# One transfer instead of two for the first tile of a streamed mixture of softmaxes, and a buffer wait moved from ScalarE to GpSimd

## The chip, the cores and the metric

The kernel runs on one core of a Trainium2 chip. The metric is device time in microseconds (us). I also give the **span** of the profiled execution, the time from its first to its last recorded work.

## The reference, cut to what matters

```python
batch, seq, vocab, num_heads = 32, 128, 4096, 4
# logits [32, 128, 4, 4096] fp32, prior [32, 128, 4] fp32
prior_probs = softmax(prior, axis=-1)
mixture = np.sum(prior_probs[..., None] * softmax(logits, axis=-1), axis=2)   # [32, 128, 4096]
```

For each of 4096 rows: four softmaxes over 4096 numbers, weighted and added. 268.5 MB are read and 67.1 MB written.

## The kernel before

The rows are worked on in U = 32 units of 128 rows, one row to a partition. A unit reads 64 KB a row (four heads of 16 KB) and writes 16 KB a row. The input tile holds two units, so unit u's load goes where unit u - 2 was.

```python
    def load(u):
        if u == 0 or u >= U - 3:
            cuts = (0, 2, 3, 4) if u == U - 1 else (0, 2, 4)
        else:
            cuts = (0, H)
        for h, to in zip(cuts, cuts[1:]):
            ld = nc.scalar.dma_start(
                out=ltile[:, u % 2, h:to], in_=lg[u // J, u % J, :, h:to, :]
            )
            if u >= 2:
                only(ld, adds[u - 2, 0] if h == 0 else exps[u - 2, to - 1])
            # ...
            for k in range(h, to):
                loads[u, k] = ld
```

`only` says what an instruction waits for. Loads are issued from ScalarE's queue, most stores from SyncE's, so they are two queues on the same 16 DMA engines (the page of the kernel before books 82.2% and 17.6% of the 16 engines' time on them). In each unit:

```python
            def exp(h, *keep):                      # ScalarE: exponential and its sum
                ex = nc.scalar.activation(es[h], lt[:, h], AF.Exp, accum_out=dsum[:, u, h : h + 1])
                keep = (loads[u, h],) + keep
                if bufd and u and h in (1, 2):      # the buffers of unit u - 1 must be free
                    keep += (adds[u - 1, 1 if h == 1 else H - 1],)
                exps[u, h] = only(ex, *keep)

            def weigh(h, n, *keep):                 # VectorE reciprocal, GpSimd product
                # ...
                return only(mul, rc, *keep)

            free = (stores[u - 2],) if bufd and u >= 2 else ()     # the output tile of unit u - 2
            # ... sets: ((0, H),) for u < U - 4, then pairs and singles of heads
            for h in range(H):
                if h == 2 and 0 < u < U - 3:
                    store(u - 1, obuf[:, (u - 1) % 2], nc.sync)
                # ...
                exp(h, *(free if sets[0][1] == H and h == H - 1 else ()))
                # ...
                mul = weigh(g, h + 1 - g, *(free if g == 0 and h < H - 1 else ()))
                for k in range(g, h + 1):           # VectorE: scale head 0, then add 1 to 3
                    # ... add(k, mul, ...)
```

So load u + 2 waits for the scaling of unit u (`adds[u, 0]`), which waits for all four exponentials of unit u.

The softmax here doesn't subtract the row's maximum and nothing guards it: scores larger than these inputs give would overflow.

## Time and profile before

| | before |
|---|---|
| time, median | 780.8 us |
| span | 779.1 us |
| moved | 335.64 MB, 431 GB/s over the span |
| VectorE, ScalarE, GpSimd busy | 66%, 61%, 1% |
| DMA engines | full from the first load to the end |

The table says that transfers are the bound: no compute engine is busy for more than two thirds of the span, and the DMA row of the profile is full.

### The profile page before, as it was taken

The numbers are of one execution on the slowest core, as the hardware profiler recorded it, in microseconds if no ns is written. First come the engines' busy times: TensorE is split into PE (matmuls) and PEld (weight loads), VectorE is DVE, ScalarE is ACT, GpSimd is POOL, SyncE is SP. The second block draws the span as 40 slices with busy tenths as digits, with TensorE's granted clock in tenths as the row PEclk, the third lists the DMA queues.
The fourth block names the chain that finished last, engine by engine and source line by source line (L and its number), as shares of the span: only waits on it lengthen the run. The fifth ranks groups of instructions, "written<-read, shape, count | busy, mean of one in ns | idle before, by whom it ended". The sixth has DMA issues, their size and how long they took to land.

```text
span 779.1 us, 620 instructions
## 1 busy us (share of the span) xinstructions
DVE 517.7 (66%) x175; ACT 472.2 (61%) x258; POOL 7.6 (1%) x41
## 2 busy tenths in 40 slices
DVE  2447865568655686556875558755577555788986
ACT  4376555765557755577555675556755567557782
POOL 0000000000000000000000000000000000000000
DMA  9999999999999999999999999999999999999998
GB/s 407 458 417 400 475 404 431 431 465 424 404 468 401 463 417 423 452 448 414 417 468 407 458 404 468 421 413 448 416 459 417 457 405 464 410 429 431 432 428 379
DMA packets 10131, 335.64 MB, mean 431 GB/s; under 512 B 1136, under 2 KB 1136, under 8 KB 1168
## 3 DMA queue, kind: packets, MB, share of 16 engines
q10 hardware_dynamic: 6048, 276.83, 82.2%
q1 hardware_dynamic: 4080, 58.79, 17.6%
q14 instruction: 3, 0.02, 0.0%
HBM read 268.50 MB, written 67.11 MB: 431 GB/s over the span
## 4 chain that ended last, share of the span: by engine, by line
DMA 60%; DVE 28%; ACT 9%; issue 2%; POOL 0%; DVEq 0%; ACTq 0%; POOLq 0%
DMA out_dram<-obuf 47%; DVE obuf L200 23%; DMA ltile<-in_logits_dram 13%; ACT ebuf L176 8%; DVE obuf L194 4%; DVE ltile L200 1%; ACT ltile L176 1%; POOL coeff L187 0%; DVE rden L185 0%; DVEq L271 0%; ACTq L111 0%; POOLq L271 0%; ACTq L176 0%
## 5 line engine op out<-in xcount | busy, mean ns | idle before, releaser
L200 DVE SCALAR_TENSOR_TENSOR obuf<-ebuf,coeff,obuf 128x4096 f32<-128x4096 f32 x90 | 403.6, 4484 | 3.8 <-POOL coeff L187 0.6
L176 ACT ACTIVATE ebuf<-ltile 128x4096 f32<-128x4096 f32 x90 | 324.1, 3601 | 33.3 <-DVE obuf L200 19.4
L176 ACT ACTIVATE ltile<-ltile 128x4096 f32<-128x4096 f32 x38 | 137.4, 3615 | 255.4 <-DMA ltile<-in_logits_dram 255.0
L185 DVE RECIPROCAL rden<-dsum 128x4 f32<-128x4 f32 (+2 forms) x37 | 6.4, 174 | 235.9 <-ACT ebuf L176 233.2
L194 DVE TENSOR_SCALAR obuf<-ltile,coeff 128x4096 f32<-128x4096 f32 x30 | 70.6, 2353 | 10.9 <-POOL coeff L187 10.9
L200 DVE SCALAR_TENSOR_TENSOR ltile<-ltile,coeff 128x4096 f32<-128x4096 f32 (+1 forms) x7 | 27.0, 3874 | 1.0 <-POOL coeff L187 0.9
L176 ACT ACTIVATION_READ_ACCUMULATOR ebuf<-ltile 128x1 f32 x90 | 16.8, 187 | 0.0
L187 POOL TENSOR_TENSOR coeff<-rden,pp 128x4 f32<-128x4 f32 (+2 forms) x37 | 7.4, 201 | 756.2 <-DVE rden L185 745.6
L176 ACT ACTIVATION_READ_ACCUMULATOR ltile<-ltile 128x1 f32 x38 | 7.1, 186 | 0.0
L194 DVE TENSOR_SCALAR ltile<-ltile,coeff 128x4096 f32<-128x4096 f32 x2 | 4.7, 2353 | 0.6 <-POOL coeff L187 0.6
L153 ACT ACT_TABLE_LOAD x1 | 1.3, 1283 | 2.2 <-issue 2.2
L151 DVE TENSOR_REDUCE pmax<-pr 32x128 f32<-32x512 f32 x1 | 0.7, 674 | 2.5 <-DMA pr<-in_prior_dram 2.5
L162 DVE STREAM_TRANSPOSE pp<-pn 32x256 f32<-32x256 f32 x4 | 1.7, 435 | 0.1
L154 DVE TENSOR_REDUCE pmax<-pr 32x128 f32<-32x512 f32 x1 | 0.7, 674 | 0.7 <-ACT pr L153 0.7
L156 DVE TENSOR_TENSOR pn<-pr,pmax 32x512 f32<-32x512 f32 x1 | 1.0, 1019 | 0.0
L155 DVE RECIPROCAL pmax<-pmax 32x128 f32<-32x128 f32 x1 | 0.9, 941 | 0.0
L153 ACT ACTIVATE pr<-pr 32x512 f32<-32x512 f32 x1 | 0.6, 628 | 0.5 <-DVE pr L152 0.5
L152 DVE TENSOR_TENSOR pr<-pr,pmax 32x512 f32<-32x512 f32 x1 | 0.7, 679 | 0.0
L260 POOL MEMSET const-bfloat16-1.0<- 128x1 bf16 x1 | 0.1, 102 | 0.0
L260 POOL MEMSET const-uint8-127<- 128x1 uint8 x1 | 0.1, 102 | 0.0
L260 POOL MEMSET const-float32-0.0<- 128x1 f32 x1 | 0.1, 99 | 0.2 <-issue 0.2
L260 POOL MEMSET const-float32-1.0<- 128x1 f32 x1 | 0.1, 99 | 0.0
## 6 DMA issues: line engine op xcount, KB each, us to landing
out_dram<-obuf SPq DMA_DIRECT2D x28, 2048.0 KB, 28.1
ltile<-in_logits_dram ACTq DMA_DIRECT2D x7, 4096.0 KB, 25.5
ltile<-in_logits_dram ACTq DMA_DIRECT2D x2, 2048.0 KB, 30.9
out_dram<-obuf ACTq DMA_DIRECT2D x2, 2048.0 KB, 26.6
out_dram<-ltile ACTq DMA_DIRECT2D x1, 2048.0 KB, 19.3
out_dram<-ltile ACTq DMA_DIRECT2D x2, 1024.0 KB, 4.8
ltile<-in_logits_dram ACTq DMA_DIRECT2D x28, 29.6
pr<-in_prior_dram SPq DMA_DIRECT2D x1, 64.0 KB, 2.5
```

The lines of the kernel that those rows point to most:

```text
L151: nc.vector.reduce_max(pmax, pr, axis=AX.X)
L152: nc.vector.tensor_sub(pr, pr, pmax.unsqueeze(2).to_broadcast([2 * G, P, H]))
L153: nc.scalar.activation(pr, pr, AF.Exp)
L154: nc.vector.reduce_sum(pmax, pr, axis=AX.X)
L155: nc.vector.reciprocal(pmax, pmax)
L156: nc.vector.tensor_mul(pn.rearrange("k h r -> k r h"), pr, pmax.unsqueeze(2).to_broadcast([2 * G, P, H]))
L162: nc.vector.transpose(pp[32 * t : 32 * (t + 1), :, :, c : c + 2 * G], pq[:, :, :, 32 * (t % 2) : 32 * (t % 2 + 1)],)
L176: ex = nc.scalar.activation(es[h], lt[:, h], AF.Exp, accum_out=dsum[:, u, h : h + 1])
L185: rc = nc.vector.reciprocal(rden[:, u, h : h + n], dsum[:, u, h : h + n])
L187: mul = nc.gpsimd.tensor_mul(coeff[:, u, h : h + n], rden[:, u, h : h + n], ppu[:, h : h + n])
L194: st = nc.vector.tensor_scalar(out=acc[:, lo:hi], in0=es[h][:, lo:hi], scalar1=coeff[:, u, h : h + 1], scalar2=None, op0=ALU.mult,)
L200: st = nc.vector.scalar_tensor_tensor(out=acc[:, lo:hi], in0=es[h][:, lo:hi], scalar=coeff[:, u, h : h + 1], in1=acc[:, lo:hi], op0=ALU.mu ...
```

## The change

Its intent: fewer and larger transfers at the start, and ScalarE freed from a wait on a store in the two units where GpSimd may take it.

```diff
     def load(u):
-        if u == 0 or u >= U - 3:
+        if u >= U - 3:
             cuts = (0, 2, 3, 4) if u == U - 1 else (0, 2, 4)
...
-                exp(h, *(free if sets[0][1] == H and h == H - 1 else ()))
+                exp(h, *(free if 4 <= u < U - 4 and h == H - 1 else ()))
...
-                mul = weigh(g, h + 1 - g, *(free if g == 0 and h < H - 1 else ()))
+                mul = weigh(g, h + 1 - g, *(free if g == 0 and not 4 <= u < U - 4 else ()))
```

## The prediction

> **What bounds the kernel now.** I read the page of the kernel before first: shares by engine, then the row of DMA slices.
>
> ```profile
> span 779.1 us, 620 instructions
> ...
> DVE 517.7 (66%) x175; ACT 472.2 (61%) x258; POOL 7.6 (1%) x41
> ...
> DMA  9999999999999999999999999999999999999998
> ...
> DMA packets 10131, 335.64 MB, mean 431 GB/s; under 512 B 1136, under 2 KB 1136, under 8 KB 1168
> ```
>
> No compute engine reaches 70%, while the DMA engines are at 9 tenths or more in 39 of 40 slices and 8 in the last. The reference has to read 268.5 MB and write 67.1 MB, and the kernel moves just that. The transfers are the bound; compute only has to issue them in time.
>
> Next, the chain of waits in order of time, for the steady rate. A piece of the middle:
>
> ```profile
> 120.33 28.15 DMA out_dram<-obuf
> 148.50 3.72 ACT ebuf L176 x2
> ...
> 152.73 2.37 DVE obuf L194
> 155.12 4.50 DVE obuf L200
> 159.64 4.50 DVE obuf L200
> 164.16 4.50 DVE obuf L200
> 168.68 28.44 DMA out_dram<-obuf
> ```
>
> The columns are start, length, what. A unit is 128 rows of 64 KB in (8.39 MB) and 16 KB out (2.10 MB), so 10.49 MB. The chain repeats every 168.68 - 120.33 = 48.35 us, and that is two units (its links go from unit u to u + 2, through the store that frees an output buffer). So 20.97 MB go in 48.35 us: 434 GB/s, or **24.17 us a unit**. The 28 us of a 2 MB store are no slow store: it shares the engines with the next unit's load. At 434 GB/s all 335.64 MB need 773.4 us of the 779.1 us span. Only some 5.7 us are start, end and lost rate, so no change that moves the same bytes can win more than that.
>
> The second number is what compute alone would need per unit. The third add of unit u frees the PSUM tile and the last buffer for the exponentials 2 and 3 of unit u + 1. The loop is therefore: three adds (13.53 us), two exponentials (about 3.72 each with the accumulator read, 7.4 together), reciprocal, GpSimd product and their gaps (103.67 + 0.19 to 104.38, 0.5 us), the scaling on VectorE (2.35 and 0.04 of gap): **23.8 us**. Compute is faster than the transfers by 0.37 us a unit. That is the rate at which a compute delay is made up.
>
> Last, the timeline of the first 60 us, where the change acts.
>
> ```profile
> 12.25 3.62 ACT L176 ACTIVATE ltile<-ltile 128x4096 f32<-128x4096 f32 x1 [7.70 <-DMA ltile<-in_logits_dram]
> ...
> 21.96 3.59 ACT L176 ACTIVATE ebuf<-ltile 128x4096 f32<-128x4096 f32 x1 [2.40 <-DMA ltile<-in_logits_dram]
> ...
> 32.18 0.33 ACTq L111 DMA_DIRECT2D ltile<-in_logits_dram  x1
> 32.18 13.53 DVE L200 SCALAR_TENSOR_TENSOR obuf<-ebuf,coeff,obuf 128x4096 f32<-128x4096 f32 x3
> 41.31 3.62 ACT L176 ACTIVATE ltile<-ltile 128x4096 f32<-128x4096 f32 x1 [12.04 <-DMA ltile<-in_logits_dram]
> ...
> 58.73 0.33 ACTq L111 DMA_DIRECT2D ltile<-in_logits_dram  x1
> ```
>
> Unit 0's first half is there at 12.2 us, its second at 21.9, unit 1 at 41.3. Load 2 is issued at 32.18, when the scaling of unit 0 has freed its buffer, 9.1 us before load 1 is in: that is the lead the change will spend.
>
> **What the Trainium skill says.** "Perfetto Trace Analysis", section DMA Optimizations: splitting a transfer may let work start sooner "if DMA engines are generally idle". Here they are not, yet the split does start ScalarE sooner (12.25 rather than 21.96); the question is whether anybody needs that. "DMA: Bandwidth & Descriptors", section Queues, rings and completion order: each engine takes turns between its queues by packets. The trace agrees: the packet records show store 0, issued at 45.74, starting its first data packet at 50.57, amid load 2's packets. Same page, section Latency and other measured facts: a first byte about 0.6 us after the issue on the queues of SyncE and ScalarE. The trace shows more: unit 0's load begins issue at 0.12 and its first packet starts at 1.29, so I take 1.2 us. Same page, section Where 436 GB/s comes from: a ceiling of 435.2 GB/s. The 434 above agrees, and leaves nothing to gain in rate.
>
> **The change part by part.**
>
> *One load for unit 0.* It removes one DMA issue (0.33 us of ScalarE's queue) and leaves bytes and order alike: 8.39 MB, then unit 1. Unit 0 should land at 21.9 us as before. ScalarE then does four exponentials after 21.9 instead of two. Unit 1 shows what that takes: from 41.31 to the end of the scaling at 58.73, 17.42 us. So load 2 is issued at 21.96 + 17.42 = **39.4 us instead of 32.18: 7.2 us later**. Now follow the transfers:
> - Load 1's last packets end at 40.4 to 40.9 us. Load 2's first can start at 39.4 + 1.2 = 40.6. So the engines idle for about 0 to 0.3 us. The lead of 9.1 us shrinks to 1.9, still about what an issue takes.
> - Unit 0's adds end at 39.4 + 13.55 = 52.9 (before 45.74), and store 0 follows. Exponential 2 of unit 1 waits for it (before: no wait, 48.52). So unit 1's scaling ends at 39.4 + 23.8 = 63.2 instead of 58.73, and load 3 is issued 4.5 us later.
> - From 40.6 the engines have load 2 and store 0, 10.49 MB: busy until 40.6 + 24.17 = 64.8. Load 3 can start at 63.2 + 1.2 = 64.4. No gap, by 0.4 us: what covers it is store 0, which now is mostly sent after load 2.
> - From there each round takes 23.8 us of compute against 24.17 of transfers, so the margin grows by 0.37 a unit. Unit 3's scaling would end at 39.4 + 3 x 23.8 = 110.8 (before 106.77), 4.0 us late, and the delay is gone after 4.0 / 0.37, some 11 units, about unit 14. From there the two kernels should look alike, the end included.
>
> So 7.2 us of delay on ScalarE cost 0 to 0.3 us of span at the first joint and perhaps 0 to 0.4 at the second.
>
> *The wait for the output tile, units 2 and 3.* It moves from the fourth exponential to GpSimd's product, which runs after that exponential anyway. Nothing is added. Before, unit 2 did not wait, and unit 3 waited this long:
>
> ```profile
> 100.14 3.62 ACT L176 ACTIVATE ebuf<-ltile 128x4096 f32<-128x4096 f32 x1 [0.36 <-DMA out_dram<-obuf]
> ```
>
> So 0.36 us at most. With the first part in, it should be 0: unit 3's fourth exponential now starts near 104 us, and store 1, issued near 76.8, should be out by about 64.8 + 24.2 = 89. Also, what ScalarE gains there while the engines are full only issues a load earlier into a full queue.
>
> Sum: 0 to 0.7 us slower, middle 0.3.
>
> **The rivals.** *The first exponential's 9.7 us delay goes straight through.* That would give 788 to 790. For it: in these first 60 us the chain goes through load 1 and unit 1's exponentials. Against it: the engines are full and load 2 still comes as load 1 ends. *The thin margins tear at every joint.* If issue to first packet were 2 us and not 1.2, the gap would be 1 us at the first joint and 0.4 at the second, then shrinking as 0.37 a unit is made up: 782 to 783. *The period does not recover*, because the exponentials' new waits make compute the bound; 23.8 against 24.17 speaks against it, and even at equality it costs nothing. *It gets faster*: the rate is below the steady one while unit 1 is worked on:
>
> ```profile
> 30.00:40.00 10.00, 9.93 (x3) 0.00 (x0) 0.00 (x0) 1.00 0.97 419
> 40.00:50.00 10.00, 5.67 (x2) 8.69 (x5) 0.00 (x0) 1.00 1.01 419
> 50.00:60.00 10.00, 3.80 (x3) 5.81 (x4) 0.20 (x1) 1.00 0.96 411
> 60.00:70.00 10.00, 9.93 (x3) 5.49 (x3) 0.00 (x0) 1.00 1.01 419
> ```
>
> The last column is GB/s. From 40 to 70 us it is 416 in the mean, 18 under 434: about 30 x 18 / 434 = 1.2 us (some of that is packets counted in the next stretch). I do not know the cause; if it is how load and store meet there, the change could win or lose up to a microsecond. Against a win: nothing shows that later stores do any harm to the rate.
>
> **Range and chances.** 780.82 + 0.3 gives 781.1. Below, the lost rate regained (-0.9); above, gaps at the first joints (+1.7): 780.0 to 782.7. Two per cent is 15.6 us, more than all the slack there is on the fast side and more than the whole delay on the slow side: 0.98 for within 2%.
>
> **What would show it right or wrong.** In the profile of the changed kernel: first exponential at about 21.9; load 2 issued at about 39.4; store 0 at about 52.9; load 3 at about 63.2; exponential 2 of units 1, 2 and 3 waiting for adds; unit 3 about 4 us later than before, unit 14 and after alike within a microsecond; bytes the same, DMA slices of 9 throughout. The prediction is wrong if the DMA share falls in a stretch between 40 and 90 us, or if the steady period is not 48.35 us for two units.

## The result, and the profile after

The changed kernel took **783.79 us** (783.47 to 784.83, six runs) against 780.78 (780.68 to 780.90): 3.0 us slower. The ratio is 1.004, 95% interval 1.0027 to 1.0053. Ratios here and below are the mean time of one kernel's runs over that of the other's of the same rounds, so not quite the ratio of the medians quoted. It is outside the predicted range of 780.0 to 782.7.

The page of the changed kernel, the same rows as in the prediction:

```profile
span 781.7 us, 622 instructions
...
DVE 517.7 (66%) x175; ACT 471.9 (60%) x258; POOL 7.6 (1%) x41
...
DMA  9999999999999999999999999999999999999998
...
DMA packets 9987, 335.64 MB, mean 429 GB/s; under 512 B 1120, under 2 KB 1120, under 8 KB 1152
```

Bytes and busy times are as before. The DMA row still shows nines: a slice is 19.5 us, so a loss of a microsecond does not show there. The timeline at the start (start, length, engine, operation, in brackets the idle time before it and what ended it; ACTq and SPq are the queues from which ScalarE and SyncE issue transfers):

```profile
22.12 3.62 ACT L176 ACTIVATE ltile<-ltile 128x4096 f32<-128x4096 f32 x1 [18.01 <-DMA ltile<-in_logits_dram]
...
39.53 0.33 ACTq L111 DMA_DIRECT2D ltile<-in_logits_dram  x1
39.54 13.52 DVE L200 SCALAR_TENSOR_TENSOR obuf<-ebuf,coeff,obuf 128x4096 f32<-128x4096 f32 x3
41.45 3.62 ACT L176 ACTIVATE ltile<-ltile 128x4096 f32<-128x4096 f32 x1 [4.83 <-DMA ltile<-in_logits_dram]
...
53.10 3.59 ACT L176 ACTIVATE ebuf<-ltile 128x4096 f32<-128x4096 f32 x1 [4.33 <-DVE obuf L200]
...
63.31 0.33 ACTq L111 DMA_DIRECT2D ltile<-in_logits_dram  x1
```

This is the predicted sequence to two tenths of a microsecond: load 2 at 39.53 (predicted 39.4), exponential 2 of unit 1 waiting for an add until 53.10, load 3 at 63.31 (63.2). So the schedule was right. But the delay did not go away. Unit 14's first exponential, in the kernel before and then in the changed one:

```profile
354.51 3.62 ACT L176 ACTIVATE ltile<-ltile 128x4096 f32<-128x4096 f32 x1 [8.39 <-DMA ltile<-in_logits_dram]
```

```profile
357.30 3.62 ACT L176 ACTIVATE ltile<-ltile 128x4096 f32<-128x4096 f32 x1 [8.39 <-DMA ltile<-in_logits_dram]
```

2.8 us late, with the same wait for the load. And the first exponential of the last unit, before and after:

```profile
749.04 3.62 ACT L176 ACTIVATE ltile<-ltile 128x4096 f32<-128x4096 f32 x1 [2.40 <-DMA ltile<-in_logits_dram]
```

```profile
751.62 3.62 ACT L176 ACTIVATE ltile<-ltile 128x4096 f32<-128x4096 f32 x1 [2.43 <-DMA ltile<-in_logits_dram]
```

From there to the end of the span it is 779.1 - 749.0 = 30.1 us in the one and 781.7 - 751.6 = 30.1 in the other. **So the whole difference of the spans is that load 31 lands 2.6 us later.** The question is why a stream of the same bytes on full engines is 2.6 us late.

### Under the averages: the records of single packets

The trace has one record for each packet on a DMA engine, and each of the 16 engines ends its part of a transfer with a 4-byte completion. ScalarE waits for the last of the 16: in all twenty traces the first exponential of the last unit starts 0.4 to 0.5 us after it. The records do not name the engine; the first 16 packets of a transfer, and its 16 completions, are taken as one for each engine. From these records (not a view of the profile, my own count):

```
first half of load 31           first engine  last engine  mean of 16  last - first
kernel before                      747.56       748.55       747.82       0.99
changed kernel                     748.90       751.17       749.65       2.27
```

The mean engine is 1.83 us late and the slowest 2.62. So two things came about: the engines **lost time together**, and they went **out of step** by more than a microsecond more than before. I call the second **skew**.

For the first, I summed idle time and the time by which packets took longer than usual (a 64 KB packet usually takes 2.42 us), divided by 16:

```
us lost per engine                                        before   changed
slow packets of load 0 at the start                         0.40      0.60
around 41 us, idle                                          0.00      0.64
around 41 us, first packets of load 2 (2.99 for 2.42)       0.00      0.57
slow packets where store 0 is issued and after, to 64 us    0.89      1.31
later (84 and 132 us)                                       0.00      0.18
sum                                                         1.29      3.30
```

The difference is 2.0 us. The first row does not count, as the mean engine ends load 1 at the same time in both kernels (40.65 and 40.64 us); without it 1.8 us are left, the 1.83 by which the mean engine is late. The largest part is the **break** in the stream around 41 us, where the engines stand idle and then send slow packets: 1.21 us.

### The profile page after: what moved, and what is told of

It reads as the page before. It is cut to its first block, busy times and chain, and to the rows that moved or that the text cites. A ratio compares the mean times of both kernels' runs of the same rounds, so it can differ in the third digit from the quotient of the medians.

```text
span 781.7 us, 622 instructions
## 1 busy us (share of the span) xinstructions
DVE 517.7 (66%) x175; ACT 471.9 (60%) x258; POOL 7.6 (1%) x41
## 4 chain that ended last, share of the span: by engine, by line
DMA 50%; DVE 34%; ACT 12%; issue 3%; POOL 0%; DVEq 0%; ACTq 0%; POOLq 0%
DMA out_dram<-obuf 40%; DVE obuf L200 28%; ACT ebuf L176 11%; DMA ltile<-in_logits_dram 10%; DVE obuf L194 5%; DVE ltile L200 1%; ACT ltile L176 1%; POOL coeff L187 0%; DVE rden L185 0%; DVEq L272 0%; ACTq L111 0%; POOLq L272 0%; ACTq L176 0%
```

## The experiments

Eighteen runs, all with correct results; three rounds each. Kernels are compared only within the same rounds. "Spread" is the time from the first to the last of an engine's completions in the first half of load 31; "slowest" is the last of them.

| run | median us | before | span | slowest | spread |
|---|---|---|---|---|---|
| before | | 780.8 | 779.1 | 748.55 | 0.99 |
| changed kernel | 783.79 | 780.78 | 781.7 | 751.17 | 2.27 |
| e1 one load only | 783.69 | 780.81 | 781.9 | 751.35 | 2.46 |
| e2 moved wait only | 780.82 | 780.81 | 778.9 | 748.34 | 0.85 |
| e3 two loads, compute late | 783.34 | 780.81 | 781.5 | 751.04 | 2.13 |
| e4 changed, load 2 in halves | 783.06 | 780.81 | 781.0 | 750.44 | 2.20 |
| e5 load 2 issued at 36.7 | 780.83 | 780.82 | 779.0 | 748.48 | 0.92 |
| e6 load 2 issued at 41.1 | 783.47 | 780.82 | 781.1 | 750.55 | 0.91 |
| e7 unit 0 in 1 + 3 heads | 781.37 | 780.82 | 779.8 | 749.35 | 1.90 |
| e8 unit 0 in four | 782.21 | 780.82 | 780.4 | 749.91 | 2.21 |
| h1 store 0 at 48.6 | 780.88 | 780.83 | 779.1 | 748.53 | 0.96 |
| h2 store 0 at 52.4 | 780.75 | 780.83 | 778.8 | 748.25 | 0.95 |
| g1 before, 16 KB packets | 786.66 | 780.83 | 784.9 | 754.35 | 1.48 |
| g2 changed, 16 KB packets | 787.73 | 780.83 | 785.8 | 755.22 | 1.46 |
| p1 store 0 at 49.5 | 781.23 | 780.80 | 779.0 | 748.52 | 0.97 |
| p2 store 0 at 49.8 | 781.04 | 780.80 | 778.8 | 748.25 | 0.90 |
| p3 e8, store 0 held | 781.62 | 780.80 | 779.1 | 748.53 | 0.91 |
| p4 e4, store 0 held | 783.17 | 780.80 | 780.6 | 750.05 | 1.46 |
| q1 store 0 at 49.1 | 781.04 | 780.80 | 779.2 | 748.66 | 1.11 |
| q2 store 0 at 48.95 | 780.76 | 780.80 | 778.9 | 748.40 | 0.90 |

In every row the span is 30.5 or 30.6 us more than "slowest". So the slowest engine's share of load 31 sets the end in all twenty programs, and the last two columns say how much of it is skew.

Each kernel has one trace, of one of its timed executions, and executions differ: e6's trace is of its fastest (782.89; the others took 783.05 to 784.23), p4's too (782.47, up to 783.76), and e1 and h2 had one execution each far above the rest (786.16 and 782.40) that left no trace. Spans are on record for every execution.

### Which part of the change: e1 and e2

```diff
 e1 (of before)
-        if u == 0 or u >= U - 3:
+        if u >= U - 3:
```

> Only the first part: unit 0 in one transfer, the waits for the output tile as before. Theory: the whole 3.0 us come from this part, so 783.8 us, with load 2 issued at 39.5 and the DMA engines partly idle between 40 and 44. Rival (the moved wait costs, because GpSimd holds back the scaling): near 780.8.

```diff
 e2 (of before)
-                exp(h, *(free if sets[0][1] == H and h == H - 1 else ()))
+                exp(h, *(free if 4 <= u < U - 4 and h == H - 1 else ()))
...
-                mul = weigh(g, h + 1 - g, *(free if g == 0 and h < H - 1 else ()))
+                mul = weigh(g, h + 1 - g, *(free if g == 0 and not 4 <= u < U - 4 else ()))
```

> Only the second part: unit 0 in two transfers, the wait of units 2 and 3 on GpSimd. Theory: 780.8 us (at best 0.4 less), as nothing there waits long. Rival (the moved wait costs): 783 to 784.

e1: 783.69 us, ratio 1.0044 (1.0028 to 1.0059). e2: 780.82, ratio 1.0001. The single load is the whole cost, the moved wait is worth nothing in either direction. In e2, unit 3's fourth exponential starts with no idle time in front of it, where 0.36 us were before; the gain led nowhere, since it only sends a load sooner into a full queue.

### The form of the transfer or the lateness of compute: e3

```diff
 e3 (of before: still two transfers for unit 0)
-                keep = (loads[u, h],) + keep
+                keep = (loads[u, h if u else H - 1],) + keep
```

> The kernel before, unit 0 in two transfers, but its first exponential waits for the second of them, so compute starts at 21.9 as in the changed kernel. Theory (lateness of unit 0's compute): 783.8 us. Rival (the form of the transfer, 64 KB rows against 32 KB, or its one completion): 780.8.

783.34 us, ratio 1.0031 (1.0014 to 1.0047), load 2 issued at 39.30, spread 2.13. Lateness of unit 0's compute is enough to bring the loss about; the number of transfers and the size of their packets are not needed.

### The break by itself: e5 and e6

These delay load 2 alone and leave unit 0's compute and store 0 as they were.

```diff
 e5 and e6 (of before; 1 in e5, 2 in e6)
-                only(ld, adds[u - 2, 0] if h == 0 else exps[u - 2, to - 1])
+                only(ld, adds[u - 2, 1 if u == 2 else 0] if h == 0 else exps[u - 2, to - 1])
```

> The kernel before, with load 2 waiting one add longer (issued at about 36.7 instead of 32.2), compute and stores on time. Theory: the issue is still ahead of load 1's end at 40.5 by more than the 1.2 us from issue to first packet, so no break and 780.8 us. Rival (any loss of lead costs in proportion): 4.5 of 7.2 us, so 782.7.

> The kernel before, with load 2 waiting two adds longer (issued at about 41.2, after load 1's last packet at 40.5), compute of unit 0 and store 0 on time. Theory: DMA engines idle for about 1.8 us around 41 and slow first packets add about 0.5, so 783.1 us; the stores alone, on time, cost nothing. Rival (the break costs nothing, late stores all): 780.8.

e5, issued at 36.72: 780.83 us, no cost, with 4.5 of the 7.2 us of lead gone. Unit 2's first exponential starts at 64.53, in the kernel before at 64.51:

```profile
36.72 0.33 ACTq L111 DMA_DIRECT2D ltile<-in_logits_dram  x1
...
64.53 3.62 ACT L176 ACTIVATE ltile<-ltile 128x4096 f32<-128x4096 f32 x1 [8.71 <-DMA ltile<-in_logits_dram]
```

e6: 783.47, ratio 1.0038 (1.0021 to 1.0054). Its timeline:

```profile
41.13 0.33 ACTq L111 DMA_DIRECT2D ltile<-in_logits_dram  x1
41.51 3.62 ACT L176 ACTIVATE ltile<-ltile 128x4096 f32<-128x4096 f32 x1 [12.33 <-DMA ltile<-in_logits_dram]
...
45.65 0.36 SPq L124 DMA_DIRECT2D out_dram<-obuf  x1
...
58.93 0.33 ACTq L111 DMA_DIRECT2D ltile<-in_logits_dram  x1
67.28 3.62 ACT L176 ACTIVATE ltile<-ltile 128x4096 f32<-128x4096 f32 x1 [11.26 <-DMA ltile<-in_logits_dram]
```

Load 2 is issued at 41.13, after load 1's last packets have ended (40.4 to 40.8); store 0 and load 3 go out as in the kernel before. The packet records show 1.69 us idle and 0.58 of slow first packets, 2.3 together. Load 31's slowest engine is 2.0 us late, the spread unchanged: in the traced execution, the fastest of four, the break cost about what it lasted (782.89, 2.1 us more than the kernel before), and compute's slack did not make it up. What the other three executions lost beyond that is not known. Lead is a threshold, not a slope: 4.5 us less of it cost nothing, 9 us less cost a break.

### The break taken away: e4

```diff
 e4 (of the changed kernel)
+        parts = ((2, 4), (0, 2)) if u == 2 else tuple(zip(cuts, cuts[1:]))
-        for h, to in zip(cuts, cuts[1:]):
+        for h, to in parts:
```

(and the first half, too, is placed ahead of unit 1's exponentials on ScalarE's queue.)

> The changed kernel, but load 2 comes in halves, heads 2 and 3 first: they need only unit 0's exponentials, so they are issued at about 36.5 instead of 39.5, ahead of load 1's end at 40.5. Theory (most of the cost is the break in the stream at 40 to 44 us, 1.2 us, with the rest from store 0 being late): 781.5 to 782.6. Rival (the break is all): 780.8. Rival (the break costs nothing, the late stores all): 783.8.

783.06 us, ratio 1.0030: a miss, above the range. The break is gone: the first half of load 2 is issued at 36.51 and its packets start the moment load 1's end, with no idle time. The mean engine gained 0.57 us against the changed kernel (749.08 against 749.65), less than the 1.21 of the break, because packets were slow at 54 to 58, 78 to 86 and 106 to 112 us. And the spread was 2.20. So a late unit 0 costs time without the break, too; but this run also sends load 2 in 32 KB packets and in another order, so it does not say how much of the changed kernel's own loss is the break.

### Less late and earlier: e7 and e8

```diff
 e7 and e8 (of e1; (0, 1, 2, 3, 4) in e8)
-            cuts = (0, H)
+            cuts = (0, 1, H) if u == 0 else (0, H)
```

> Unit 0 in transfers of one head and three heads: the second lands at 21.9 with three exponentials to do, so load 2 is issued at about 35.9, store 0 at about 49.4. Theory (a break in the stream costs, a shorter lead does not): within 0.5 us of 780.8. Rival (late stores cost in proportion, 3.7 of 7.3 us): 782.3.

> Unit 0 in four transfers of one head: one exponential left when the last lands at 21.9, so load 2 is issued at about 28.6 and store 0 at about 42. Theory (break in the stream): no break either way, so 780.8 us within 0.4. Rival (earlier stores win in proportion): 779.3.

e7: 781.37 us, ratio 1.0008 (0.9993 to 1.0022), just outside my half microsecond, and not clear of the noise (its four spans are 778.9 to 780.2). e8: 782.21, ratio 1.0018 (1.0003 to 1.0033): **slower, although load 2 (28.71) and store 0 (42.26) are issued earlier than in the kernel before**, and neither theory said so. In both, the mean engine is late by 0.1 to 0.3 us only (747.94 and 748.11 against 747.82) and the spread is doubled. Here skew is nearly the whole cost. The records of store 0's first packets show how the engines parted:

```
                 first packet of store 0 on the 16 engines
before           all 16 at 50.6 to 51.0
e7               4 at 52.8 to 53.0, 12 at 55.2 to 55.6
e8               1 at 45.8, 15 at 48.0 to 48.4
```

The groups are 2.4 us apart, one 64 KB load packet: some engines took the store one load packet sooner than the others.

### Is a late store 0 the cause? h1 and h2

```diff
 h1 and h2 (of before; exps[1, 2] in h2, where the store also comes one head later in the text)
-        stores[u] = only(st, adds[u, H - 1])
+        stores[u] = only(st, adds[u, H - 1], *([exps[1, 1]] if u == 0 else []))
```

> The kernel before, with store 0 alone held back from 45.7 to about 48.5 us; loads and compute on time, no break in the stream. Skew theory (where store 0's packets meet load 2's 64 KB packets decides whether the 16 DMA engines fall out of step; the slowest engine then sets every landing): spread of load 2's 16 completions over 1.5 us against 0.4, and 781.3 to 782.3 us. Rival (only the break and slow packets cost, the spread is a bystander): 780.8.

> As the last, with store 0 held back to about 52.1, near the 53.1 of the changed kernel. Skew theory: spread of load 2's completions 2 us or more and kept to the end, 781.5 to 782.7 us, with the break still absent. Rival (break only): 780.8.

Misses for the theory as I had put it: store 0 at 48.57 and 52.37 cost nothing (780.88 and 780.75 us), all engines took it in one group, and load 2's completions were spread by 0.39 and 0.48 us (later 1.1 us for two loads of h2, which went back to 0.5). One of h2's four executions took 782.40; it left no trace. Lateness of store 0 alone is not what skews.

### Smaller packets: g1 and g2

Padding after each head's row makes the loads go in 16 KB packets.

```diff
 g1 (of before) and g2 (of the changed kernel)
-    ltile = cpool.tile([P, 2, H, V], FP32, name="ltile")
+    ltile = cpool.tile([P, 2, H, V + 8], FP32, name="ltile")     # used as [..., :V] everywhere
```

> The kernel before, with 32 bytes of padding after each head's row in the input tile, so that loads go in 16 KB packets like the stores. For the next run to be compared with. Stores then take turns one to one and land in about 10 us. The engines stay full, so 780 to 782.

> The changed kernel with the same padding. Skew theory (a skew is worth up to one load packet, 2.4 us at 64 KB, 0.6 at 16 KB): only the break at 40 us is left, so 0.7 to 1.5 us slower than the padded kernel before, with the completions of a load within 1 us of each other. Rival (the break carries the whole cost): 3 us slower, as without padding.

g1: 786.66 us, g2: 787.73. Both are slower than the kernel before (ratios 1.0074 and 1.0087, g1 above the range I gave, with stores that landed in 14.3 us and not in about 10; why g1 is slower I did not look into), but their difference is 1.1 us in place of 3.0, the mean engine of load 31 0.92 us late and the slowest 0.87, the spread alike (1.48 and 1.46). With small packets the change brought no skew to the end, as expected. The test isn't clean: the idle part of the break shrank too, from 0.64 to under 0.1 us, so the fall from 3.0 to 1.1 is not skew alone.

### What sets the skew off: p1, p2, q1, q2, and p3, p4

The theory after e7 and e8: a store reaching the engines just as they change from one load packet to the next is taken in two groups. To place store 0 finely, tiny GpSimd products hold it.

```diff
 p1 (of before; 4 products in p2, 2 in q1, 1 in q2; in p3, of e8, 5 after adds[0, H - 1];
     in p4, of e4, 3 after adds[0, H - 1])
+        hold = [adds[u, H - 1]]
+        if u == 0:
+            for i in range(3):
+                m = nc.gpsimd.tensor_mul(scratch, rden[:, 0, :], rden[:, 0, :])
+                only(m, *([exps[1, 1]] if i == 0 else []))
+            hold.append(m)
-        stores[u] = only(st, adds[u, H - 1])
+        stores[u] = only(st, *hold)
```

> The kernel before, with store 0 alone held by three tiny GpSimd products to about 49.3 us, just about 1 us ahead of the moment (50.1 to 50.5) when the engines change from one 64 KB load packet to the next. Boundary theory: some engines take store 0 one load packet sooner than the others, so its first packets start in two groups 2.4 us apart, load 2's completions spread by 1.5 us or more, and the time is 781.3 to 782.3 us. Rival (skew comes only with a break or with shifted compute): one group, 780.8, like the stores at 45.7, 48.6 and 52.4.

> As the last with one more tiny product, some 0.2 us later (about 49.5). Boundary theory: near the edge, so a part of the engines or all of them one packet later: between 780.8 and 782.3, with a spread over 1.5 us only if the first store packets are in two groups. Rival: 780.8.

> As p1 and p2, with two tiny products: store 0 issued at about 49.16. p1 (49.48) and p2 (49.80) came after the edge and h1 (48.57) before it; in e7 a store issued at 49.29 was taken in two groups. So 49.16 should be on the edge. Boundary theory: first packets of store 0 in two groups 2.4 us apart, load 2's completions spread by 1.2 us or more, span up by 0.5 to 1.3 us over the 779.1 of before. Rival (shifted compute is needed too): one group, 779.1.

> As q1 with one tiny product: store 0 issued at about 48.84, just ahead of the edge or on its first part. Boundary theory: most or all engines in the early group (first store packet near 52.9), with a spread only if there are two groups; span 779.1 if one group. A control for the tiny products themselves.

p1 and p2 missed the edge (issued at 49.48 and 49.80, all 16 engines in one late group) and showed no lasting skew. q1 hit it: issued at 49.10, eight engines took store 0 at 53.2 to 53.4 and eight at 55.9. In q2 (48.95) thirteen took it at 53.1 to 53.5. So arrival at the change of packets does split the engines, without a break and without shifted compute. **But it did not cost anything:** in q1 load 2's completions were spread by 1.05 us, by load 4 this was 0.44, and the span is 779.2. The engines in front fell back: against the kernel before, the first completion lost 0.61 us from load 3 to load 4, the last nothing. The step from split to lasting skew is missing in the theory, and the prediction of 0.5 to 1.3 us failed.

> The kernel with unit 0 in four transfers (782.2, one engine of 16 out of step, store 0 at 42.3) with store 0 held to about 43.4, clear of the change of packets at 43.0 to 43.4 less 1 us. Boundary theory: all engines in one group, spread under 0.7, and 780.8 us. Rival (the early compute itself costs): 782.2.

p3 holds e8's store 0 from 42.26 to 43.58, and that is all. The beginning of e8 and then of p3:

```profile
42.26 0.36 SPq L124 DMA_DIRECT2D out_dram<-obuf  x1
...
67.66 3.62 ACT L176 ACTIVATE ltile<-ltile 128x4096 f32<-128x4096 f32 x1 [11.72 <-DMA ltile<-in_logits_dram]
```

```profile
43.58 0.36 SPq L130 DMA_DIRECT2D out_dram<-obuf  x1
...
65.11 3.62 ACT L183 ACTIVATE ltile<-ltile 128x4096 f32<-128x4096 f32 x1 [9.24 <-DMA ltile<-in_logits_dram]
```

A store sent 1.3 us **later** brought load 2 in 2.55 us **sooner**: all 16 engines took the store in one group (48.2 to 48.6), load 2's completions were spread by 0.32 us and not 2.82, and the span fell from 780.4 to 779.1, that of the kernel before (all four executions: 779.5 to 780.4 in e8, 779.0 to 779.2 in p3). This shows that in e8 the skew was the cost, and that the place of store 0 made it. The time fell less, from 782.21 to 781.62: in p3 it is 2.5 us above the span (781.56 for the profiled run), in the kernel before 1.8. e8 (2.1) and p1 (2.2) have some of this, too, q2 has not; I do not know what these tenths outside the span are.

> The changed kernel with load 2 in halves (783.1: no break, but completions spread by 2.2 us) with store 0 held from 52.95 to about 53.7, off the change of packets by half a 32 KB packet. Boundary theory: spread under 1 us and 781 to 782. If the spread stays at 2 us the edge was missed or something else skews here: 783.

p4: 783.17 us against e4's 783.06. In the traces the spread fell from 2.20 to 1.46 and the span from 781.0 to 780.6, but p4's trace is of its fastest execution; the median spans of the four are alike (781.2 and 781.1). Inconclusive; the mean engine, late by 1.2 us in both traces, is most of it.

No run beat the kernel before: the best, h2 and q2, are equal to it within a tenth of a microsecond.

## Why the prediction was wrong

**Right:** the bound; the schedule of unit 0 to 3 (load 2 at 39.53 for 39.4, store 0 at 53.09 for 52.9, load 3 at 63.31 for 63.2, scaling of unit 3 ended at 110.84 for 110.8); that lead as such is worth nothing (e5: 4.5 us of it given up for nothing); that the moved wait is worth nothing (e2); that there is no gap when load 3 starts; and "within 2%".

**The step that failed** is "Load 2's first can start at 39.4 + 1.2 = 40.6. So the engines idle for about 0 to 0.3 us", and with it the sum "0 to 0.7 us slower". It was mis-sized twice, and a term was missing.

- *Issue to first packet.* Here 1.2 us was the fastest engine only. In the changed kernel load 2 is issued at 39.53 and its first packets start at 40.71 to 42.64 on the 16 engines, 1.77 us after the issue in the mean. Load 1's last packets ended at 40.34 to 41.07. Mean idle: 0.64 us. In the trace of before, load 0's first packets start at 1.29 to 2.20, and I took the 1.29. But 1.2 us is no bad figure for engines that stand idle: in e6, issued after load 1's end, it was 0.97 to 1.51, 1.16 in the mean. It is too small for an issue close before the end of the last load, 0.8 us before the first engine's here: 1.77 us in the mean, 1.78 in e1 and 1.94 in e3. Why is open.
- *First packets after a break are slow:* 2.99 us for 2.42, another 0.57. Load 0's first packets in the trace of before had the same (about 0.4 us more than the rest), and I did not count them. Break in all: 1.21 us where I had 0 to 0.3. That a break costs about what it lasts is shown by e6.
- *The missing term: the 16 engines out of step.* A load lands when the slowest engine is done. I treated the engines as one pipe of 434 GB/s. In the changed kernel the slowest engine is late by 2.62 us and the mean by 1.83, so 0.8 of the 2.6 us is skew, by this account; no run took the skew out of the changed kernel. Where it comes from is not shown. The restart is uneven: twelve engines start load 2 at 40.7 to 41.2, four at 42.1 to 42.6. But e1, with a restart from 40.7 to 41.8, ends with more skew (2.46), and e4 gets 2.20 without a break; store 0's first packets, too, are 2.4 us apart here (58.1 to 60.5) against 0.4 in the kernel before. At load 2's end the spread is 3.1 us; at the last load it is still 2.3. From load 8 to load 28, and again at load 31, the first engine is 1.3 us later than in the kernel before, the mean engine 1.8 and the last 2.6 to 2.8: nobody catches up. "From there the two kernels should look alike" was wrong for the break and the skew together: unit 14 is 2.8 us late, and compute's 0.37 us a unit of slack makes up delays of compute, not of the stream.
- *The rest*, 0.4 us in the mean engine, is slow packets where store 0 meets load 2 (1.31 us against 0.89). I saw the loss of rate there before and named it as a rival; its cause I still do not know.

**Of the rivals**, "the thin margins tear" with 2 us from issue to first packet came nearest, 782 to 783. Its gap at the first joint came (0.64 us idle, not 1), its gap at the second did not, and it had neither the slow packets nor the skew: that its number is near is in part luck.

**Open:** why the restart is late and uneven; what makes the skew of the changed kernel (no run has the later stores late and all else on time); why a split of the engines lasted in e7 and e8 and healed in q1; and why packets slow down as the first store comes in. That the traces differ by 2.6 us and the medians by 3.0 is mostly the choice of executions: over the six runs of the changed kernel the median span is 781.85, against 779.0 for the kernel before in e1's call: 2.85 us.

## What to carry to other kernels

Here, with the DMA engines as the bound, the early half of load 0 was worth nothing as speed-up of compute, but it was worth the lead it gave load 2. The next transfer must be issued well before the last one ends: 3.6 us before the first engine's last packet was enough (e5), 0.8 us was not, what lies between was not measured, and more lead gained nothing. Compare the completions of the engines one by one, since a full DMA row can hide engines that are out of step, and every load here landed with the slowest. With differences of a microsecond, a small shift of one store can move the time as much as the change under study, so make the change in more than one way before believing a trend.

## What the Trainium skill lacked or had wrong

- "DMA: Bandwidth & Descriptors", section Latency and other measured facts, has about 0.6 us to the first byte on these queues. Here, counted from the start of the issuing instruction, the first packets came 1.2 to 2.1 us later for load 0 of the kernel before (issued at 0.12, packets from 1.29 to 2.20), 1.0 to 1.5 us on idle engines in e6, and 1.2 to 3.1 us in the changed kernel, where load 2 was issued (39.53) while the engines still had load 1's last packets (to 40.34 to 41.07).
- The same page does not say that the first packet after a break is slow: 2.99 us for 2.42 at 64 KB, in the mean of 16 engines (load 2 of the changed kernel; the same in e6).
- The same page, section Queues, rings and completion order, says that the queues take turns by packets. It does not say what follows for the share of a queue: beside loads in 64 KB packets a 2 MB store took 28.1 us in the median, beside loads in 16 KB packets 14.3 (g1).
- No page has that the 16 engines can go out of step and stay so for the rest of the program: completions of one load spread by 2.3 us at the end of the changed kernel against 1.0 in the kernel before, 0.8 us of the loss by the account above.
